# Program order through the first half's q/k stage, and rotation tables made earlier, in an RG-LRU and attention block

## The chip, the cores and the metric

The kernel runs on one core of a Trainium2 chip. The core has a matrix engine (TensorE, PE in the profile, with its weight loads listed apart as PEld), a vector engine (VectorE, DVE), a scalar engine (ScalarE, ACT), a general one (GpSimd, POOL) and an engine that mostly issues transfers (SyncE, SP). They share an on-chip memory; PE writes into a small accumulator memory of eight banks (PSUM). DMA queues move data between the on-chip memory and the chip's main memory (DRAM). Each engine works through its own list of instructions in order, and waits on semaphores for the others.

The metric is the device time of one execution, in microseconds (us). A kernel's time is the median of several runs; beside them one execution is recorded by the hardware profiler.

## The reference

One layer over 2048 positions of width 1024, in float32. The input is normed and modulated, then projected by one weight matrix to eight parts of 1024 columns:

```python
h = rms_norm(x, g_norm[l]) * (1.0 + scale[:, None, :]) + shift[:, None, :]
proj = h @ w_in[l]
x_rnn, z_rnn, q, k, v, z_attn, g_r, g_a = jnp.split(proj, IN_SPLITS, axis=-1)
xc = causal_depthwise_conv(x_rnn, conv_w[l], conv_b[l])
hr = rg_lru(xc, w_a[l], b_a[l], w_x[l], b_x[l], lam[l], positions)
y_rnn = (hr * jax.nn.silu(z_rnn)) @ w_out_rnn[l]
qh = apply_partial_rope(q, cos, sin); kh = apply_partial_rope(k, cos, sin)
o = dilated_attention_mixture(qh, kh, v)
y_attn = (o * jax.nn.silu(z_attn)) @ w_out_attn[l]
merged = sigmoid(g_r + bg_r) * y_rnn + sigmoid(g_a + bg_a) * y_attn
x = x + gate[:, None, :] * (merged @ w_o[l])
```

and a last norm. The rotation (rope) turns the first 32 of each head's 128 columns by the angles positions x inv_freq; its cosine and sine are the same for all 8 heads and for q and k.

## The kernel before

**Tiles and halves.** Activations lie transposed: 128 columns of a result by 512 positions, which is a bank. The 2048 positions are four banks, worked in two halves (f = 0 and 1) of two banks each. Each half has a values stage (v, written as it is used later), a recurrent stage and a q/k stage. Attention, the merge and the output follow after both halves.

**Products.** Float32 is had from PE by splitting every operand in a high and a low part and adding three matmuls. A *pair* is a 256-column piece of the weight matrix times the two banks of the half; it is done by a Strassen scheme with 7 *products* in place of 8. A product is 12 matmuls of 128x512 (4 blocks of the contraction, three parts each) on one weight operand of 128x4x128 in two parts. The products' results go to the PSUM tiles X, Z, W, V and Y and are added up on DVE and ACT (u1, u2, u3, then one eviction for each quarter of the pair); line 440 is such an eviction. A pair's last product is put off into the next pair (`last_product`).

**Operands.** In the first half the weights come from DRAM as raw tiles R (SP, line 243, four to ten products ahead of use), DVE forms the Strassen sums s1 and s2, ACT rounds the high part (line 154) and POOL takes the low part (line 160) into one of seven tiles S, four products ahead; the split operand is also stored to the DRAM array sD (ACT's queue). In the second half the same operands are loaded from sD straight into S (SP, line 307), up to seven ahead, one more each time a product has been issued.

**Stages.** The recurrent stage of a half has 8 recurrent pairs (`recurrent`: conv, two small gate matmuls per block with the weights w_a and w_x, scan, product with the silu gate) and 14 other pairs between them, by the list `others`: gate pairs (z_attn, g_r, g_a; `gate_pairs`) and 2 of the plain pairs. That is 22 pairs, 154 products. The q/k stage has the two *rotated* pairs, which hold the first 32 columns of each head of q and of k, and 4 *plain* pairs, which hold the other columns: 42 products. The rotated results get a lane shuffle (DVE), a product with the cosine table Ct (POOL) and with the sine table St (DVE), and an addition, and go to the arrays qT and kT.

**What lies beside the products.** Before the rotated pairs the q/k stage makes the tables (`rotary_tables`): positions to angles, reduction by 2 pi in 13 exact subtractions (line 890), two sines on ACT, a repeat to 128x512 (rep, line 905), four transposes on PE (line 907) and a copy into Ct or St; rep, transposes and copy four times. In the first half the stage also loads and norms bank 2 of x (line 490), whose transposed and split operands are built during the last pair (`next_even`, line 511); in the second half it makes the residual gate.

**Order.** The program is written in one order; a scheduler then moves instructions on each engine, by its own model of the machine. Exempt from it is only the first half's recurrent loop, which stands in program order on all engines:

```python
with nullcontext() if f else tc.manual_schedule():
    for m in range(KT):
        recurrent(rp, bigr, f, m)
```

Inside it, work that should lie some products later is hung on a counter of products (`steps_after`, the dictionaries `late` and `after_prod`), and `pump` issues the operand events that have come due.

## Time and profile before

| | |
|---|---|
| runs | 2305.05, 2310.1, 2318.68 us (median 2310.1) |
| profiled execution | 2306.3 us, its span 2304.5 |
| granted TensorE clock, mean | 0.987 |

A row of the stage table gives a stretch of the span, then its length, the busy time and count of instructions of PE, weight loads, DVE, ACT and POOL in it, the granted clock (1.00 is full speed), the DMA engines' busy share and what they moved in GB/s. A row of an engine's timeline gives the start, the busy length, the line, the operation with out<-in, and in brackets how long the engine had waited ahead of it and for whom. A row of the chain of waits gives a start, a length and what ran; it follows the work that ended last back through what released each step. A row of DMA issues ends in the size of one and the median time from issue to landing.

### The profile page before, as it was taken

The numbers are of one execution on the slowest core, as the hardware profiler recorded it, in microseconds if no ns is written. First come the engines' busy times: TensorE is split into PE (matmuls) and PEld (weight loads), VectorE is DVE, ScalarE is ACT, GpSimd is POOL, SyncE is SP. The second block draws the span as 40 slices with busy tenths as digits, with TensorE's granted clock in tenths as the row PEclk, the third lists the DMA queues.
The fourth block names the chain that finished last, engine by engine and source line by source line (L and its number), as shares of the span: only waits on it lengthen the run. The fifth ranks groups of instructions, "written<-read, shape, count | busy, mean of one in ns | idle before, by whom it ended". The sixth has DMA issues, their size and how long they took to land.

```text
span 2304.5 us, 34059 instructions
## 1 busy us (share of the span) xinstructions
PE 2230.6 (97%) x11461; PEld 1867.7 (81%) x11461; DVE 1333.6 (58%) x2442; ACT 1242.3 (54%) x2416; POOL 964.6 (42%) x734
## 2 busy tenths in 40 slices
PE   8999999999979999999999999899999998989998
PEld 4998888888858998778888877788888897978886
DVE  4828676867574705343534462466667777667443
ACT  4737666866633636555644411567678777534211
POOL 2457666766545334232111021455556565433000
PEclk9999999999999999999999999999999999999999
DMA  7366888787959388998676779988888887799542
GB/s 264 107 224 245 286 281 280 252 292 272 320 173 311 106 281 303 322 318 297 203 230 229 252 235 301 274 250 277 267 248 247 229 255 233 231 322 284 161 128 92
DMA packets 427284, 569.20 MB, mean 247 GB/s; under 512 B 71943, under 2 KB 292835, under 8 KB 426085
## 3 DMA queue, kind: packets, MB, share of 16 engines
q1 hardware_dynamic: 389268, 447.27, 63.0%
q10 hardware_dynamic: 37648, 119.70, 13.3%
q8 instruction: 91, 1.49, 0.3%
q14 instruction: 85, 0.69, 0.1%
q0 software_dynamic: 192, 0.05, 0.0%
HBM read 355.08 MB, written 211.82 MB: 246 GB/s over the span
## 4 chain that ended last, share of the span: by engine, by line
PE 55%; DMA 8%; DVE 4%; ACT 3%; issue 2%; SPq 2%; POOL 1%; ACTq 0%; POOLq 0%; DVEq 0%
PE pj L146 12%; PE pq L146 8%; PE X L146 8%; PE V L146 7%; PE sc L146 4%; PE o L146 4%; PE Z L146 4%; PE W L146 4%; PE Y L146 3%; DMA wD<-s 1%; PE pT L1299 1%; DMA S<-sD 1%; PE pT L1312 1%; PE pg L146 1%; DMA gaT<-ev 1%
## 5 line engine op out<-in xcount | busy, mean ns | idle before, releaser
L146 PE MATMUL pj<-yh,S 128*128 128x512 f32 x1024 | 370.3, 406 | 4.3 <-DMA S<-wD 2.1
L146 PE MATMUL X<-T,S 128*128 128x512 f32 x1344 | 335.0, 398 | 5.2 <-ACT t L925 2.1
L146 PE MATMUL V<-T,S 128*128 128x512 f32 x1344 | 331.7, 395 | 6.3 <-DVE ev L440 2.7
L160 POOL TENSOR_TENSOR S<-R,S 128x512 fp32r<-128x512 f32 x168 | 251.8, 1510 | 189.6 <-ACT S L154 66.7
L146 PEld LDWEIGHTS X<-T,S 128*128 128x128 f32 x1344 | 254.7, 190 | 66.7 <-ACT t L925 3.1
L146 PEld LDWEIGHTS V<-T,S 128*128 128x128 f32 x1344 | 252.2, 188 | 66.9 <-DVE t L440 5.2
L146 PEld LDWEIGHTS pj<-yh,S 128*128 128x128 f32 x1024 | 194.8, 190 | 41.4 <-DVE fg L1506 2.5
L146 PE MATMUL pj<-yl,S 128*128 128x512 f32 x512 | 202.3, 395 | 0.0
L1215 ACT ACTIVATE pp<-pp,st 128x256 f32<-128x256 f32 (+3 forms) x256 | 133.9, 524 | 112.1 <-DVE st L1214 111.0
L160 POOL TENSOR_TENSOR S<-s,S 128x512 fp32r<-128x512 f32 x84 | 125.9, 1499 | 122.8 <-ACT S L154 96.4
L146 PE MATMUL Z<-T,S 128*128 128x512 f32 x672 | 166.8, 396 | 4.8 <-ACT S L154 4.5
L146 PE MATMUL W<-T,S 128*128 128x512 f32 x672 | 166.0, 395 | 0.3 <-POOL S L160 0.3
L146 PE MATMUL Y<-T,S 128*128 128x512 f32 x672 | 166.2, 395 | 0.0
L146 PEld LDWEIGHTS Z<-T,S 128*128 128x128 f32 x672 | 126.6, 189 | 35.3 <-ACT S L154 4.9
L146 PEld LDWEIGHTS W<-T,S 128*128 128x128 f32 x672 | 126.3, 188 | 30.8 <-issue 0.9
L146 PEld LDWEIGHTS Y<-T,S 128*128 128x128 f32 x672 | 126.2, 188 | 30.3 <-issue 0.9
L812 DVE SCALAR_TENSOR_TENSOR xc<-xr,par,xc 128x512 f32<-128x512 f32 x96 | 92.6, 964 | 78.6 <-ACT xc L806 76.9
L163 DVE TENSOR_TENSOR ptl<-pT,pth 128x384 fp32r<-128x384 f32 (+1 forms) x160 | 97.8, 628 | 64.9 <-ACT pth L154 62.7
L154 ACT ACTIVATE S<-R 128x512 fp32r<-128x512 f32 x168 | 102.3, 623 | 58.6 <-DMA R<-in_w_in_dram 28.2
L1279 ACT ACTIVATE pp<-pp,M 128x256 f32<-128x256 f32 (+3 forms) x256 | 117.9, 523 | 8.8 <-DVE M L1403 8.8
L1214 DVE CUSTOM_DVE_ANT_0 pp<-sc,msk 128x256 f32<-128x256 f32 (+3 forms) x256 | 105.1, 449 | 28.4 <-PE sc L146 25.5
L160 POOL TENSOR_TENSOR vh<-vraw,vh 128x256 fp32r<-128x256 f32 (+1 forms) x64 | 67.4, 1053 | 104.7 <-ACT vh L154 95.0
(357 smaller groups left out, 4697.4 us busy)
## 6 DMA issues: line engine op xcount, KB each, us to landing
sD<-S ACTq DMA_DIRECT2D x196, 512.0 KB, 4.0
S<-sD SPq DMA_DIRECT2D x196, 512.0 KB, 5.6
S<-wD SPq DMA_DIRECT2D x99, 512.0 KB, 5.6
R<-in_w_in_dram SPq DMA_DIRECT2D x136, 256.0 KB, 4.2
wD<-s ACTq DMA_DIRECT2D x64, 256.0 KB, 5.9
T<-in_w_mod_dram SPq DMA_DIRECT2D x8, 1024.0 KB, 11.6
vN<-ev SPq DMA_DIRECT2D x64, 128.0 KB, 2.4
zaT<-ev SPq DMA_DIRECT2D x32, 256.0 KB, 4.6
```

Source lines behind the costliest of these rows:

```text
L146: last_mm[0] = nc.tensor.matmul(o, lhsT=l, rhs=r, start=st, stop=sp, **kw).ins
L154: nc.scalar.activation(o, i, AF.Copy)
L160: nc.gpsimd.tensor_tensor(o, i, h.bitcast(F32), ALU.subtract)
L163: return nc.vector.tensor_tensor(o, i, h.bitcast(F32), ALU.subtract).ins
L812: nc.vector.scalar_tensor_tensor(xc, xr[:, i : i + CH], cw(i), xc, ALU.mult, ALU.add)
L1214: nc.vector.tensor_tensor_reduce(pdst, s_ps, mask, 1.0, 3e38, ALU.add, ALU.min, m_)
L1215: nc.scalar.activation(pdst, pdst, AF.Exp, bias=m_, scale=-1.0, accum_out=l_)
L1279: nc.scalar.activation(pp, pp, AF.Copy, scale=w)
L1299: nc.tensor.transpose(pt[:, c0 + j * P : c0 + (j + 1) * P], pp[i][:, k * P : (k + 1) * P], ident)
L1312: nc.tensor.transpose(pt[:, c * P : (c + 1) * P], pp[:, half * P : (half + 1) * P], ident)
```

## The change

**Order.** The first half's program order no longer ends with the recurrent loop. It is entered at the same place and closed after the q/k stage's last pair. The second half and all else stay with the scheduler.

**Tables.** `rotary_tables` is called at the start of each half's recurrent stage and hangs its work on products: the angles at product 24, then one small group of DVE operations after each product, and the four repeats, transposes and copies at products 56, 76, 91 and 111 and shortly after. The copies go through the tiles `ev` that the gates also use, and to a DRAM array tabD; the q/k stage loads Ct and St from there (`load_tables`).

**Steps of the q/k stage.** What the scheduler placed is now hung on products by hand: the scaling of q one product after the eviction, the shuffle and the turn one and two after that; bank 2's norm in parts (`next_norm`: four squares, one square root for all four, four scalings); the transposes and builds of bank 2 one step apart; the residual gate over some 30 products.

**Small ones.** The recurrent blocks' gate weights are loaded into an `ev` tile in place of one of their own (gr_); the rotated results have one t0 tile more in the first half and one t1 more in both; `others` places the same 14 pairs otherwise (1, 2, 2, 1, 2, 2, 1, 3 behind the eight recurrent ones, before 1, 2, 2, 2, 1, 2, 2, 2); `rstd` works on several rows at once, in as many operations.

```diff
+    def rstd_first(ss):
+
+        nc.vector.tensor_scalar(ss[:, 0], ss[:, 0], 1.0 / D, EPS, ALU.mult, ALU.add)
+        nc.scalar.activation(ss[:, 1], ss[:, 0], AF.Sqrt)
...
         def load_weights():
-            w["raw"] = T(rp, [P, 2, P], F32, "gr_", bufs=1)
+            w["raw"] = T(rp, [P, 4, P], F32, "ev", bufs=3)[:, :2]
...
-    def rotary_tables(qp, f):
+    def rotary_tables(rp, f):
...
+        def piece(q, i):
+
+            def repeat():
+                src = v[("co", "an")[i]]
+                v["rep"] = T(rp, [P, 4, 8, 16], F32, "ev", bufs=3)
+                nc.vector.tensor_copy(v["rep"][:], src[:, 4 * q : 4 * q + 4, :].unsqueeze(2).broadcast_to([P, 4, 8, 16]))
+
+            def turn():
+                v["pt"] = T(pg, [P, 4, P], F32, "pg")
+                for r in range(4):
+                    nc.tensor.transpose(v["pt"][:, r, :], v["rep"][:, r].rearrange("p a b -> p (a b)"), ident)
+
+            def store():
+                t = T(rp, [P, CH], F32, "ev", bufs=3)
+                pt = v["pt"][:].rearrange("p r j -> p (r j)")
+                if i == 0:
+                    nc.scalar.activation(t[:], pt, AF.Copy)
+                else:
+                    nc.vector.tensor_scalar(t[:], pt, cs[:, K_SG : K_SG + 1], None, ALU.mult)
+                nc.sync.dma_start(tabD[f, i, :, q * CH : (q + 1) * CH], t[:])
+
+            return repeat, turn, store
+
+        at_, base = TABLES, n_prod[0]
+        for fn in (angles, None, products, *reduce(TWO_PI * 4096, 7, 8), *reduce(TWO_PI, 11, 5), quarter, sines):
+            if fn:
+                after_prod.setdefault(base + at_, []).append(fn)
+            at_ += 1
+
+        for x, (q, i) in enumerate((q, i) for q in range(2) for i in range(2)):
+            for d, fn in zip((0, 2, 3), piece(q, i)):
+                after_prod.setdefault(base + PIECES[x] + d, []).append(fn)
...
-    NT0 = (3, 5)
+    NT0, NT1 = (4, 5), 3
...
-            if qs != 1.0:
-                nc.scalar.activation(t[:], t[:], AF.Copy, scale=qs)
+        steps_after(n_prod[0], ((1, lambda: nc.scalar.activation(t[:], t[:], AF.Copy, scale=qs)),))
+        return 2
...
+                steps_after(n_prod[0], ((wait, shuffle), (wait + 1, add)))
...
-    others = [1 + (m % 4 > 0) for m in range(KT)]
+    others = [1, 2, 2, 1, 2, 2, 1, 3]
...
+    def next_norm():
+
+        xs = load_x(xp, 2, "x", 2)
+        ss = T(xp, [P, 3, 4], F32, "ss")
...
+        for r in range(4):
+            later(5 + r, lambda r=r: square(r))
+            later(11 + 2 * r, lambda r=r: nc.vector.tensor_scalar(xs[r], xs[r], ss[:, 1, r : r + 1], None, ALU.mult))
+        later(9, lambda: rstd_first(ss))
+        later(10, lambda: rstd_last(ss))
+        return xs
...
+        rotary_tables(rp, f)
...
-        with nullcontext() if f else tc.manual_schedule():
-            for m in range(KT):
+        order = ExitStack()
+        if f == 0:
+
+            order.enter_context(tc.manual_schedule())
+        n = 0
+        for m in range(KT):
...
-        tabs = rotary_tables(qp, f)
+        tabs = load_tables(qp, f)
...
-            x0 = load_x(xp, 2, "x", 2)
-            norm_x(xp, x0)
+            x0 = next_norm()
         rotated_pairs(qp, f, *tabs)
...
+        order.close()
         pools.close("qp")
```

Three places show the order as it now stands. The first is DVE in the first half's q/k stage, where the first rotated outputs (tiles t) are turned. Before (rep, St and co belong to the tables, line 942 and 943 are the turn, 440 an eviction):

```order
L905 COPY rep_5791<-co_5781 128x512
L905 COPY rep_5799<-an_5759 128x512
L913 TENSOR_SCALAR St_5789<-pg_5798,cs_60 128x512
L905 COPY rep_5807<-co_5781 128x512
L942 TENSOR_TENSOR t_1030_5993<-t_1030_5993,St_5789 128x512
L943 TENSOR_TENSOR t_1030_5993<-t_1030_5993,t_1029_5992 128x512
L905 COPY rep_5815<-an_5759 128x512
L440 TENSOR_TENSOR t_1039_6069<-V_5940,u_1016_5914 128x512
```

And now (451 is an eviction, 1007 the shuffle, 1012 and 1013 the turn):

```order
L451 TENSOR_TENSOR t_1022_5927<-V_5906,u_1018_5904 128x512
L1007 STREAM_SHUFFLE t_1029_5968<-t_1022_5927 128x512
L1007 STREAM_SHUFFLE t_1030_5971<-t_1026_5951 128x512
L451 TENSOR_TENSOR t_1033_5981<-Y_5953,u_1018_5904 128x512
L1012 TENSOR_TENSOR t_1029_5968<-t_1029_5968,St_5828 128x512
L1013 TENSOR_TENSOR t_1029_5968<-t_1029_5968,t_1022_5927 128x512
```

The tables' work is gone from between the turns, and an eviction stands between a shuffle and its turn.

The second place is SP at the start of the same stage. Before, with the positions (line 875) and x (490) among the raw weights R:

```order
L243 DMA R_1033_6020<-in_w_in_dram 128x4x96
L875 DMA pi_5755<-in_positions_dram 128x2x4
L490 DMA x_5825<-in_x_dram 128x2048
L490 DMA x_5827<-in_x_dram 128x2048
L243 DMA R_1043_6098<-in_w_in_dram 128x4x64 x2
```

And now, with the tables (975) and x (501):

```order
L975 DMA Ct_5827<-tabD 128x1024
L975 DMA St_5828<-tabD 128x1024
L501 DMA x_5834<-in_x_dram 128x2048
L501 DMA x_5836<-in_x_dram 128x2048
L254 DMA R_1011_5874<-in_w_in_dram 128x4x32 x4
L254 DMA R_1021_5924<-in_w_in_dram 128x4x64 x2
```

The raw weights that stood ahead of x now stand behind it and behind two tables.

The third place is SP in the second half's recurrent stage, where the fourth recurrent block's gate weights are loaded (lines 766 and 767) among the split weights S. Before:

```order
L307 DMA S_1466_8877<-sD 128x1024
L766 DMA gr__1585_9502<-in_w_a_dram 128x128
L767 DMA gr__1585_9502<-in_w_x_dram 128x128
L1030 DMA gaT<-ev_8883 128x512
L307 DMA S_1470_8897<-sD 128x1024
```

And now (783 and 784; 957 stores a piece of the tables):

```order
L318 DMA S_1584_9491<-sD 128x1024
L783 DMA ev_9528<-in_w_a_dram 128x128
L784 DMA ev_9528<-in_w_x_dram 128x128
L957 DMA tabD<-ev_9533 128x512
L1102 DMA zaT<-ev_9476 128x512
L318 DMA S_1592_9523<-sD 128x1024
```

The gate weights go into a tile of the shared ring, with a store of the tables behind them.

More of the change, by code (lines that the diff above doesn't have):

```diff
@@ L1035, in gate_pairs, with later, load, add @@
                 yield
+    def later(d, fn):
+        late.setdefault(n_prod[0] + d, []).append(fn)
     def residual_gate(ep):
         acc = T(ep, [P, D], F32, "gacc")
-        for k in range(KT):
-            t = T(ep, [P, D], F32, "gw", bufs=2)
-            nc.sync.dma_start(t[:], w_mod[0, k * P : (k + 1) * P, 2 * D : 3 * D])
+        row = T(ep, [1, D], F32, "grow")
+        nc.sync.dma_start(row[:], b_mod[0:1, 2 * D : 3 * D])
+        w = {}
+        def load(k):
+            w[k] = T(ep, [P, D], F32, "gw", bufs=2)
+            nc.sync.dma_start(w[k][:], w_mod[0, k * P : (k + 1) * P, 2 * D : 3 * D])
+        def add(k):
+            t = w.pop(k)
             if k == 0:
```

211 lines of the change are left out of this document (121 added, 90 removed).

## The prediction

> **What bounds the kernel now.** I read the first part of the page, then the table by stages, then TensorE's (PE's) own timeline in the stage that loses time, then the chain of work that ended last.
>
> ```profile
> span 2304.5 us, 34059 instructions
> PE 2230.6 (97%) x11461; PEld 1867.7 (81%) x11461; DVE 1333.6 (58%) x2442; ACT 1242.3 (54%) x2416; POOL 964.6 (42%) x734
> ```
>
> PE is the bound, with 73.9 us of idle time. Where that lies is in the stages (columns: stretch, length, busy us and count of PE, weight load, DVE, ACT, POOL; granted clock; DMA share; GB/s):
>
> ```profile
> 150.00:595.00 445.00, 445.00 (x1918) 360.89 (x1917) 322.56 (x338) 304.72 (x488) 305.77 (x207) 1.00 0.79 273
> 595.00:620.00 25.00, 24.63 (x107) 19.66 (x106) 11.05 (x13) 15.85 (x23) 14.06 (x10) 1.00 1.01 325
> 645.00:660.00 15.00, 10.83 (x50) 8.62 (x51) 9.39 (x14) 2.98 (x5) 7.10 (x6) 0.89 0.43 143
> 660.00:685.00 25.00, 18.41 (x70) 14.06 (x69) 20.09 (x27) 4.12 (x7) 13.71 (x10) 0.86 0.60 183
> 596.00:745.00 149.00, 134.62 (x587) 106.77 (x587) 91.14 (x156) 59.56 (x99) 79.28 (x58) 0.97 0.82 266
> 745.00:842.00 97.00, 94.37 (x780) 93.95 (x779) 44.50 (x78) 49.72 (x87) 40.29 (x26) 0.98 0.51 155
> 842.00:1000.00 158.00, 157.12 (x677) 126.58 (x676) 70.35 (x86) 85.98 (x137) 53.53 (x41) 1.00 0.93 317
> 1000.00:1050.00 50.00, 46.47 (x200) 37.06 (x199) 20.79 (x27) 25.32 (x41) 15.45 (x13) 1.00 1.00 345
> 1296.00:1424.00 128.00, 125.45 (x540) 98.89 (x538) 59.90 (x108) 21.82 (x37) 17.37 (x12) 1.00 0.83 269
> ```
>
> 150 to 595 is the first half's recurrent stage, which already stands in program order: PE never idles in it. 596 to 745 is the first half's q/k stage, ordered by the scheduler: 14.4 us idle, clock down to 0.86. 745 to 842 are the second half's values, 842 to 1296 its recurrent stage, 1296 to 1424 its q/k stage. The change touches these alone; the attention and output stages hold the rest of the idle time. PE in the q/k stage of the first half, with the waits in brackets:
>
> ```profile
> 597.00 2.95 PE L146 MATMUL V<-T,S 128*128 128x512 f32 x12
> ...
> 643.80 0.73 PE L146 MATMUL X<-T,S 128*128 128x512 f32 x2 [1.85 <-ACT S L154]
> 645.80 0.95 PE L907 MATMUL pg<-cs,rep 128*128 128x128 f32 x4 [1.27 <-DVE rep L905]
> ...
> 659.10 3.07 PE L146 MATMUL V<-T,S 128*128 128x512 f32 x12 [1.09 <-DVE t L440]
> 666.67 1.22 PE L146 MATMUL Z<-T,S 128*128 128x512 f32 x2 [4.50 <-ACT S L154]
> 669.99 4.57 PE L146 MATMUL X<-T,S 128*128 128x512 f32 x12 [2.09 <-ACT t L925]
> ...
> 739.29 0.60 PE L511 MATMUL pg<-cs,x 128*128 128x128 f32 x4
> 739.65 2.62 PE L146 MATMUL X<-S,T 128*128 128x256 f32 x20
> 742.10 2.94 PE L146 MATMUL V<-T,S 128*128 128x512 f32 x12
> ```
>
> PE waits for split weights (S), for the tables' copies (rep) and for evictions (t). The chain says what made them late, and what an undisturbed product costs:
>
> ```profile
> 591.19 3.69 DMA R<-in_w_in_dram
> 603.62 5.70 DMA R<-in_w_in_dram
> ...
> 619.51 11.15 DMA x<-in_x_dram
> ...
> 959.02 8.03 DMA gaT<-ev
> ...
> 1019.21 9.69 DMA S<-sD
> ...
> 1055.69 2.79 PE Z L146 x12
> ```
>
> **The change, part by part.**
>
> *The order of the first half's q/k stage.* The V of 597.00 is the last of the recurrent stage's 154 products; 42 follow, and the V of 742.10 is the last. 43 products at 2.79 us are 120.0 us. Between them stand 16 table transposes and 28 of the next bank at 0.09 (739.65 less 739.29, by four), 4.0 us, and 23 value matmuls at 0.12 (742.10 less 739.65, by 20), 2.8 us: 126.8 us of clean work. It took 742.10 + 2.79 - 597.00 = 147.9 us. So 21.1 us are lost here: 14.4 idle, and 6.7 of slow clock. That is the most this part can give; PE's work is the same before and after.
>
> In the order on DVE shown with the change, the rotated outputs (t) no longer stand behind the tables' copies (rep), and one product's eviction (line 451) stands ahead of the turn of the one before. On SP, also shown there, the loads of x stood behind the raw weights of the next three operands; now the k pair's last raw weights (R_1011) and the next pair's stand behind two tables and all of x, and x itself waits on SP until PE has left the recurrent stage's memory.
>
> That is the new wait. Sizes and times to landing:
>
> ```profile
> sD<-S ACTq DMA_DIRECT2D x196, 512.0 KB, 4.0
> gaT<-ev SPq DMA_DIRECT2D x32, 256.0 KB, 3.7
> x<-in_x_dram SPq DMA_DIRECT2D x2, 1024.0 KB, 8.8
> ```
>
> Over the two rotated pairs (14 products, 39.1 us) the queues carry 14 x 512 KB of split weights, 8 x 256 raw, 2048 of x, 1024 of tables (2 of 128x1024 f32) and 8 x 256 of outputs: 14336 KB, 14.7 MB. At the 345 GB/s of the row 1000 to 1050 that is 42.6 us, 3.5 too long; at the 325 of 595 to 620, 45.2, 6.1 too long. Against it stands the lead: a weight is split four products (11.2 us) ahead of its use, so lateness up to that does not reach PE. Bounds: 0, and 10 us if the squares of x block ACT in order with the splits behind them. I take 3, near the lower end, since both rates keep the lateness inside the lead. This part: -21.1 + 3 = -18.1 us.
>
> *The tables, now in the recurrent stages.* Per half, by these rows:
>
> ```profile
> L890 DVE SCALAR_TENSOR_TENSOR an<-kk,an x26: 267/286/1114, 629.4 to 1326.7; 128x128 f32<-128x128 f32 x26
> L905 DVE COPY rep<-co x4: 417/417/1491, 644.3 to 1337.7; 128x512 f32<-128x512 f32 x4
> L898 ACT ACT_TABLE_LOAD x1 | 1.3, 1283 | 0.0
> ```
>
> 13 subtractions at 0.286 are 3.7 us, 4 copies 1.7, some 12 more small ones at no more than 0.29, 3.5, and two evictions under 0.8, 1.6: 10.5 us of DVE, spread over products 24 to 114. ACT gets up to two table loads (2.6) and four short operations (under 2). DVE is busy 322.56 of 445 us there and ACT 304.72, so both lie beside PE. PE's 16 transposes (1.4 us) move with them and are in the clean work above, so they cancel. The pieces use the ring of three ev tiles of the gates: a copy may stand for a gate's store to land, 3.7 us on DVE; the accumulators it evicts are wanted again no sooner than two products (5.6 us) later. I take 0; if that cover were gone, 4 x 3.7 = 15; I keep 4, one wait, as the upper end. The eight small stores and the four loads (2 MB more each way over both halves) lie beside the rest.
>
> *The second half.* It stays with the scheduler. Its q/k stage loses 2.55 us idle, and loses the tables' 10.5 us of DVE too; I take -2 (-2.5 to +3). The gate weights' spread (line 1041's loads) and the changed pair order cost nothing that a row shows: same transfers, same products, and DVE has 68 us free. In its recurrent stage the recurrent block's weights come into the ev ring instead of a tile of their own. The order on SP, third place shown with the change, has the fourth such block. The load now also waits for the store that last used its ev tile, and the next split weights, one per product, stand behind it on SP. Seven are loaded ahead, so a single wait is covered, except where DMA is full, at 842 to 1050 (share 0.93 and 1.00), where PE already idles 4.4 us. I take +2 (0 to 12). The values at 745 to 842: the last builds and POOL's splits stand as close as before; 0 (-3 to +3). The merged norm (one Sqrt for four) drops a few DVE operations of 0.2 us, at nothing.
>
> Sum: -18.1 + 0 - 2 + 2 = -18.1 us. On the profiled execution's 2306.3 us (span 2304.5 and 1.8 around it) that is 2288.2. The runs' median, 2310.1, lies 3.8 above that execution, so the forecast for a median is 2292.0.
>
> The clock is the second part of the prize: after the 4.50 us wait the X of 669.99 took 4.57 us where others take 2.95, at a granted 0.86. [...]
>
> **The rivals.**
>
> *Half of it stays, because the stage is bound by its transfers.* For: the chain ahead of 643.80 is DMA of raw weights and of x, and the change puts 1 MB more into it. Against: at 645 to 685 the queues moved only 143 and 183 GB/s while PE idled. At the 266 GB/s of the whole stage 14.7 MB take 55.2 us, 16.1 over; less none to 11.2 us of lead, that is 5 to 16 instead of 3. With 11 the time is 2300: no measurable change.
>
> *Slower: SP blocks in the second half.* Place: the ev ring ahead of the S loads at 842 to 1050, where four of the eight recurrent blocks load weights. A store there takes up to 8.03 us (the chain's gaT). Four such waits reaching PE whole are 32 us, less the 2 counted: 2292 + 30 = 2322. For: full queues there, a wait of 9.69 us on S in the chain. Against: the scheduler placed the load after the S that PE needs next, and seven stand ahead. It is slower by more than the bound once each wait costs PE over 7.9 us (18.1 + 11.6 + 2, by four).
>
> **How the numbers follow.** A measurement here tells 0.5% from nothing, 11.6 us. The forecast, 2292, holds 0.63; the half gain, 2300, 0.23; the blocked queue, 2322, 0.14. The first is faster, the second mostly within 0.5%, the third slower. The range: from 2279 (21.1 + 2.5 + 3 + some 4 of the runs' scatter below 2310.1) to 2307, which takes the forecast with its upper ends (+7 and +4) and all but the worst of the half gain, and leaves out the blocked queue and a few tails.
>
> **What would show it.** In the profile after: the first half's q/k stage 19 to 21 us shorter with a granted clock of 1.00 and PE idle under 3 us; no PE wait for rep; the recurrent stage still 445 of 445. Wrong would be: PE waiting for S behind ACT's squares of x; DVE's shuffle waiting for qT stores; PE idle at 842 to 1050 well over 4.4 us behind S loads; or the values' stage growing by what the q/k stage gave.

## The result, and the profile after

The changed kernel takes 2323.6 us (median of 14 runs, 2319.2 to 2330.0); the kernel before, run beside it, 2309.4 (14 runs, 2300.9 to 2318.7). The ratio is 1.0065, with a 95% interval of 1.0052 to 1.0078. The change made the kernel about 14 us slower, where the forecast said 18 us faster.

The head of the page of the changed kernel:

```profile
span 2322.0 us, 34101 instructions
PE 2233.7 (96%) x11459; PEld 1868.9 (80%) x11461; DVE 1347.5 (58%) x2424; ACT 1238.5 (53%) x2412; POOL 971.1 (42%) x734
```

PE's work is the same, 2233.7 us where it was 2230.6; the span is 17.5 us longer. PE's idle time grew by 14.4 of them, from 73.9 to 88.3 us; the other 3.1 are matmuls that ran longer. To see where it went, both kernels are cut at the same events on PE's own timeline. Of the kernel before: the first product of the first half, the first of the second half, and the first matmul of the attention part. (Where a row counts fewer than the 12 matmuls of a product, the edge of the view cut it.)

```profile
147.81 2.48 PE L146 MATMUL X<-T,S 128*128 128x512 f32 x10
...
842.28 2.94 PE L146 MATMUL X<-T,S 128*128 128x512 f32 x12
...
1424.52 0.47 PE L146 MATMUL pj<-yh,S 128*128 128x512 f32 x1 [0.83 <-issue]
```

The same events after, with the last product of the recurrent stage (609.47; before it was 597.00) and the last one of the first half (750.04; before 742.10) between them:

```profile
150.61 2.94 PE L151 MATMUL X<-T,S 128*128 128x512 f32 x12
...
609.47 2.94 PE L151 MATMUL V<-T,S 128*128 128x512 f32 x12
...
750.04 3.02 PE L151 MATMUL V<-T,S 128*128 128x512 f32 x12
...
849.41 0.85 PE L151 MATMUL X<-T,S 128*128 128x512 f32 x3
...
1445.64 0.47 PE L151 MATMUL pj<-yh,S 128*128 128x512 f32 x1 [0.83 <-issue]
```

The differences of these starts (a product is 2.79 us long) give the account:

| stretch | before | after | difference |
|---|---|---|---|
| up to the first product | 147.8 | 150.6 | +2.8 |
| first half's recurrent stage | 449.2 | 458.9 | +9.7 |
| first half's q/k stage | 147.9 | 143.4 | -4.5 |
| second half's values | 97.4 | 96.6 | -0.8 |
| second half's recurrent and q/k stages | 582.2 | 596.2 | +14.0 |
| attention and output | 880.0 | 876.4 | -3.6 |

The first and the last row are code that the change doesn't touch; in the kernels below that leave the start alone the first lies between 147.6 and 150.6, and the last lies between 872.0 and 882.1 in all of them. Each row is one profiled execution, so 3 us in the first row and 10 in the last are no difference. The stretches between scatter less. The first half's recurrent stage takes 458.9 to 459.9 us in the five kernels that have it as changed (changed, e4, e5, e6, e8). The second half has its instructions in the same order on PE, DVE, ACT and POOL in changed, e4 and e16, and takes 596.2, 598.4 and 597.0. A difference of about 2 us there is not read as one.

The q/k row is not what it seems: most of its 4.5 us is work that now stands elsewhere. The clean work of that stage, counted as in the prediction, was 126.8 us. The 16 table transposes went to the recurrent stage (1.4 of its +9.7 us). Of bank 2's 28 transposes 24 now stand ahead of the last product, and of the 23 value matmuls 10, so the clean work is 123.4 us. Of 147.9 us, 21.1 were lost before; of 143.4, 20.0 are lost now (15.0 idle, the rest slow matmuls). The stage loses nearly as much time as before. The values' -0.8 has the 2.0 us of work in it that moved there.

PE's waits in these stretches of the changed kernel:

```profile
255.79 3.06 PE L151 MATMUL V<-T,S 128*128 128x512 f32 x12 [1.34 <-DVE ev L451]
271.15 4.61 PE L151 MATMUL X<-T,S 128*128 128x512 f32 x12 [3.94 <-ACT u L384]
...
647.94 2.47 PE L151 MATMUL V<-T,S 128*128 128x512 f32 x5 [7.01 <-DVE t L451]
...
677.05 5.18 PE L151 MATMUL V<-T,S 128*128 128x512 f32 x12 [7.50 <-ACT S L159]
...
903.65 4.60 PE L151 MATMUL V<-T,S 128*128 128x512 f32 x12 [3.78 <-DVE ev L451]
...
1033.60 1.09 PE L948 MATMUL pg<-cs,ev 128*128 128x128 f32 x4 [3.67 <-DVE ev L943]
...
1371.19 4.61 PE L151 MATMUL V<-T,S 128*128 128x512 f32 x12 [2.40 <-DVE t L451]
```

In the first half none of the waits of before is there any more, but others came: the recurrent stage, which had none, waits for evictions and for ACT where the tables' steps stand, and the q/k stage waits twice for 7 us. In the second half's products PE idles 14.5 us where it idled 7.5.

**The first half's recurrent stage.** The stretch of 55 us in which the reduction of the angles lies, before, and then after, there with its first 30 us by themselves (columns as in the table of stages):

```profile
222.00:277.00 55.00, 55.00 (x239) 44.59 (x238) 39.30 (x43) 40.23 (x65) 37.92 (x27) 1.00 0.86 300
```

```profile
222.00:252.00 30.00, 29.71 (x129) 23.79 (x128) 29.30 (x39) 20.62 (x31) 16.98 (x12) 1.00 0.72 244
222.00:277.00 55.00, 49.43 (x205) 39.07 (x204) 47.20 (x62) 37.03 (x55) 28.67 (x20) 0.97 0.73 244
```

and DVE's groups of the changed kernel in it (busy, mean ns of one, idle before):

```profile
L921 DVE SCALAR_TENSOR_TENSOR an<-kk,an 128x128 f32<-128x128 f32 x13 | 10.8, 835 | 0.3
...
L866 DVE TENSOR_TENSOR t<-t,gi 128x512 f32<-128x512 f32 x2 | 1.4, 688 | 5.6 <-ACT t L862 5.6
```

The 13 subtractions (line 921) took 835 ns each where the row that priced them had 286, 10.8 us instead of 3.7. They came up to three after one product; DVE was busy for 29.30 of the 30 us from 222 to 252, and the evictions (line 451) stood behind them. (DVE's one long idle time, 5.6 us ahead of line 866, waits for ACT.) Their spread in this half (shortest, median and longest in ns, first and last start in us):

```profile
L921 DVE SCALAR_TENSOR_TENSOR an<-kk,an x13: 278/1262/1378, 236.8 to 256.6; 128x128 f32<-128x128 f32 x13
```

**The first half's q/k stage.** SP, the row of x among the DMA issues, then ACT, at the first wait:

```profile
621.85 3.41 SPq L501 DMA_DIRECT2D x<-in_x_dram  x2
```

```profile
x<-in_x_dram SPq DMA_DIRECT2D x2, 1024.0 KB, 12.8
```

```profile
634.68 1.06 ACT L1154 ACTIVATE hf<-x 128x1024 bf16<-128x1024 f32 x1 [6.86 <-DMA sD<-S]
635.65 0.19 ACT L1154 ACTIVATION_READ_ACCUMULATOR hf<-x 128x1 f32 x1
635.74 0.62 ACT L993 ACTIVATE t<-t 128x512 f32<-128x512 f32 x1
```

The first square of x (line 1154) begins 12.8 us after the load of x was issued, which is the median landing of that load in this stage (12.8, where it was 8.8 before). ACT stands there for 6.86 us; the row names another transfer, the time is that of x. Behind it stand the scaling of q (line 993) and the splits; behind the scaling, on DVE, the turn and then the eviction that PE waits for at 647.94. At the second wait it is DVE itself:

```profile
673.07 1.56 DVE L1013 TENSOR_TENSOR t<-t,t 128x512 f32<-128x512 f32 x1
674.56 1.74 DVE L299 TENSOR_TENSOR s<-R,s 128x512 f32<-128x512 f32 x1
676.22 0.68 DVE L451 TENSOR_TENSOR t<-V,u 128x512 f32<-128x512 f32 x1
```

DVE is busy for 40.5 of the 44 us from 636 to 680, and from 639.15 on it waits for nothing. The sum at 674.56 makes the operand that ACT splits at 676.4 and PE wants since 669.5.

### The profile page after: what moved, and what is told of

The parts are those of the page before. It is cut to its first block, busy times and chain, and to the rows that moved or that the text cites. A ratio compares the mean times of both kernels' runs of the same rounds, so it can differ in the third digit from the quotient of the medians.

```text
span 2322.0 us, 34101 instructions
## 1 busy us (share of the span) xinstructions
PE 2233.7 (96%) x11459; PEld 1868.9 (80%) x11461; DVE 1347.5 (58%) x2424; ACT 1238.5 (53%) x2412; POOL 971.1 (42%) x734
## 3 DMA queue, kind: packets, MB, share of 16 engines
q8 instruction: 91, 1.49, 0.3%
## 4 chain that ended last, share of the span: by engine, by line
PE 50%; DMA 9%; DVE 4%; ACT 3%; issue 2%; POOL 1%; SPq 1%; ACTq 0%; DVEq 0%; POOLq 0%
PE pj L151 11%; PE pq L151 8%; PE X L151 7%; PE V L151 7%; PE o L151 3%; PE Y L151 3%; PE sc L151 3%; PE Z L151 3%; PE W L151 3%; DMA R<-yaT 1%; DMA vraw<-vN 1%; DMA R<-oT 1%; PE pT L1419 1%; PE pg L151 1%; DMA wD<-s 1%
## 5 line engine op out<-in xcount | busy, mean ns | idle before, releaser
L151 PE MATMUL V<-T,S 128*128 128x512 f32 x1344 | 338.7, 401 | 22.6 <-DVE t L451 9.6
L151 PEld LDWEIGHTS V<-T,S 128*128 128x128 f32 x1344 | 257.6, 193 | 86.5 <-ACT S L159 7.9
```

The source lines that it names most:

```text
L151: last_mm[0] = nc.tensor.matmul(o, lhsT=l, rhs=r, start=st, stop=sp, **kw).ins
```

## The experiments

For each run: where the cuts above fall, in us, with the median of its runs and its ratio to the kernel before on the same chip (whose medians there were 2305.8 to 2307.3).

| kernel | first product at | first half's products | values | second half | rest | median | ratio, 95% interval |
|---|---|---|---|---|---|---|---|
| before | 147.8 | 597.1 | 97.4 | 582.2 | 880.0 | 2309.4 | |
| changed | 150.6 | 602.2 | 96.6 | 596.2 | 876.4 | 2323.6 | 1.0065 (1.0052-1.0078) |
| e1 no tables | 150.3 | 591.6 | 96.6 | 586.9 | 875.8 | 2308.4 | 1.0007 (0.9991-1.0023) |
| e2 e1, own gate tile | 148.5 | 590.5 | 96.6 | 585.4 | 876.9 | 2301.3 | 0.9983 (0.9968-0.9998) |
| e3 pairs as before | 147.6 | 599.4 | 96.6 | 598.4 | 876.8 | 2322.2 | 1.0079 (1.0057-1.0100) |
| e4 x later | 148.4 | 596.9 | 96.6 | 598.4 | 874.0 | 2316.9 | 1.0058 (1.0042-1.0075) |
| e5 scheduler in q/k | 148.2 | 598.3 | 95.8 | 597.7 | 881.5 | 2322.3 | 1.0064 (1.0045-1.0083) |
| e6 e4, cosine on DVE | 150.4 | 592.7 | 96.6 | 594.4 | 875.2 | 2312.1 | 1.0024 (1.0012-1.0035) |
| e7 no sines | 150.6 | 596.2 | 96.6 | 598.3 | 880.9 | 2323.7 | 1.0076 (1.0061-1.0091) |
| e8 second half's tables as before | 148.2 | 602.9 | 96.6 | 589.5 | 878.5 | 2316.3 | 1.0041 (1.0025-1.0056) |
| e9 tables in the values stages | 156.5 | 590.5 | 102.5 | 582.9 | 877.3 | 2310.3 | 1.0019 (1.0005-1.0033) |
| e10 e9, repaired | 156.6 | 581.9 | 103.2 | 578.5 | 881.9 | 2301.4 | 0.9976 (0.9961-0.9991) |
| e11 e10, scheduler in q/k | 157.1 | 584.7 | 102.4 | 575.9 | 880.0 | 2303.5 | 0.9980 (0.9963-0.9997) |
| e12 before, tables in the values stages | 155.9 | 587.9 | 101.9 | 578.8 | 881.2 | 2306.6 | 1.0004 (0.9983-1.0026) |
| e13 no reduction | 148.0 | 592.8 | 96.7 | 588.8 | 876.6 | 2306.8 | 1.0012 (0.9997-1.0027) |
| e14 no pieces | 148.4 | 600.4 | 96.7 | 601.3 | 882.1 | 2322.9 | 1.0067 (1.0042-1.0092) |
| e15 e10, tables at the start | 180.5 | 584.4 | 97.2 | 579.2 | 872.0 | 2315.1 | 1.0035 (1.0019-1.0050) |
| e16 reduction spread | 149.2 | 593.2 | 96.6 | 597.0 | 880.5 | 2314.5 | 1.0030 (1.0019-1.0042) |
| e17 e16, repaired | 150.4 | 585.2 | 97.3 | 592.4 | 879.0 | 2299.6 | 0.9972 (0.9958-0.9986) |
| e18 e17, second half's tables as before | 147.9 | 586.2 | 98.9 | 581.5 | 882.1 | 2296.7 | 0.9952 (0.9936-0.9967) |

The first half's products are two stages, and the q/k stage holds different work from kernel to kernel. Its clean work is 43 products at 2.79 us, with the transposes at 0.09 and the value matmuls at 0.12 that the trace has in it; what is left is lost.

| kernel | recurrent stage | q/k stage | clean work | lost |
|---|---|---|---|---|
| before | 449.2 | 147.9 | 126.8 | 21.1 |
| changed | 458.9 | 143.4 | 123.4 | 20.0 |
| e1 | 448.7 | 142.9 | 123.4 | 19.5 |
| e4 | 459.9 | 136.9 | 123.4 | 13.6 |
| e5 | 459.8 | 138.6 | 124.3 | 14.2 |
| e6 | 458.9 | 133.8 | 123.4 | 10.4 |
| e10 | 448.7 | 133.1 | 122.9 | 10.3 |
| e11 | 448.7 | 136.0 | 124.2 | 11.8 |
| e12 | 449.2 | 138.7 | 122.1 | 16.6 |
| e16 | 451.0 | 142.2 | 123.4 | 18.8 |
| e17 | 450.9 | 134.3 | 122.9 | 11.4 |
| e18 | 450.8 | 135.4 | 123.4 | 12.0 |

### Are the tables dear, and where?

```diff
-        rotary_tables(rp, f)
...
-            nc.sync.dma_start(t[:], tabD[f, i])
+            nc.sync.dma_start(t[:], xv[i, 0])
```

> The changed kernel without the making of the rotation tables: all steps of rotary_tables and the stores to tabD are left out, and Ct and St are loaded from rows of x, so q and k are rotated wrongly. Theory A (the tables' small steps and their two sines delay evictions on DVE and ACT in both recurrent stages): the first half's recurrent stage loses its 9.7 us, the second half some 8 to 12 of its 14, and the kernel is at 2303 to 2308. Theory B (the second half is slower by the gate weights' shared tile or by the new order of pairs): the first half still gives back 8 to 10 us, the second half no more than 3, and the kernel is at 2311 to 2316.

The first half's products take 10.6 us less, the second half's stages 9.4 less. Nearly all of the first half's gain is in the recurrent stage, 448.7 us in place of 458.9. That is theory A in both halves, with the median (2308.4) just above its range. In each half 1.4 us of it are the 16 transposes themselves.

```diff
-            w["raw"] = T(rp, [P, 4, P], F32, "ev", bufs=3)[:, :2]
+            w["raw"] = T(rp, [P, 2, P], F32, "gr_", bufs=1)[:]
```

> As the kernel without tables (they are left out here too, and q and k rotated wrongly), and the gate weights again in a tile of their own (gr_) in place of the shared ev ring. Theory A: within 3 us of the kernel without tables. Theory B by the shared tile: 5 to 10 us faster than that kernel, all of it in the second half's recurrent stage.

The stretches fell by 1.2 us in the first half and 1.5 in the second, no more than the same code scatters, so no cost of the shared tile is shown by them. The median fell by 7.1, from 2308.4, of which these stretches explain less than half; the rest is unexplained.

```diff
-    others = [1, 2, 2, 1, 2, 2, 1, 3]
+    others = [1, 2, 2, 2, 1, 2, 2, 2]
```

> The changed kernel with the order of pairs of before (1, 2, 2, 2, 1, 2, 2, 2). Theory A: within 5 us of the changed kernel, 2319 to 2329. Theory B by the order of pairs: the second half gives back 8 us or more, and the kernel is at 2310 to 2316.

The order of pairs gives nothing back in the second half (598.4).

```diff
-        tabs = load_tables(qp, f)
+        tabs = tables_here(qp, f) if f else load_tables(qp, f)
```

(`tables_here` is the rotary_tables of before, and rotary_tables is called in the first half only.)

> The changed kernel with the second half's tables made in its q/k stage as before, the first half's as in the change. Theory A (the second half pays for its early tables): its stages come from 596 to 586 to 589 us, the kernel at 2310 to 2315. Rival (the second half pays for the shared gate tile and the new steps): 593 us or more, 2317 or more.

The second half came to 589.5, just outside the 586 to 589 of theory A: 6.7 of its 14.0 us were its early tables.

### Which part of the tables?

```diff
             for tag in ("an", "co"):
-                nc.scalar.activation(flat(tag), flat(tag), AF.Sin)
+                pass
```

> The changed kernel without the two sines in each half (the tables then hold angles, and q and k are rotated wrongly); the repeats, transposes and copies stay. Theory E (the sines' own table load and the one back to the gates' function hold ACT, and with it the release of an accumulator): the 3.9 us wait at 271 and the slow product behind it go, 5 to 6 us of the first half's recurrent stage, and 5 to 8 us of the second half's; the kernel at 2309 to 2314. Rival (DVE's small steps or the pieces' ev tiles): no more than 4 us in all, 2318 to 2324.

Theory E held for a third of the first half's loss: the wait at 271 fell from 3.94 to 2.12 us and the slow product behind it went (3.05 us in place of 4.61), 3.5 us of the first half's 6.0 being in the recurrent stage. The second half gave nothing, and the median is the rival's, 2323.7.

```diff
-        for fn in (angles, None, products, *reduce(TWO_PI * 4096, 7, 8), *reduce(TWO_PI, 11, 5), quarter, sines):
+        for fn in (angles, None, products, quarter, sines):
```

> The changed kernel without the 13 subtractions and their multiples in each half (angles are clipped, not reduced, so q and k are rotated wrongly); sines and pieces stay. If the DVE steps carry the rest: the first half gives back 4 to 6 us, the second 3 to 8, the kernel at 2310 to 2317. If not: under 2 us in each half, 2318 to 2325.

```diff
-        for x, (q, i) in enumerate((q, i) for q in range(2) for i in range(2)):
-            for d, fn in zip((0, 2, 3), piece(q, i)):
-                after_prod.setdefault(base + PIECES[x] + d, []).append(fn)
```

> The changed kernel without the four repeats, transposes, copies and stores in each half; the reduction and the sines stay, and Ct and St are rows of x (rotation wrong). If the pieces carry the second half's loss (a transpose waits there 3.7 to 5.4 us for its copy, which waits for an ev tile): the second half gives back 5 to 8 us, the first 1.4 to 3, the kernel at 2312 to 2317. If not: under 3 us in each half, 2318 or more.

It is the reduction. Without it the first half gives back 9.5 us, more than expected, and the second 7.4, though the sines and the pieces are still there (the sines some 30 us earlier, at 233.46 in place of 263.28, and PE has no wait in that stage). Without the pieces the first half gives back 1.8 and the second nothing (601.3), though the transpose that waited at 1033 is gone. The sum of the parts left out one by one is not the whole, since each shortens the same queues.

```diff
-            return [multiple] + [lambda i=i: subtract(ccs[i : i + 3]) for i in range(0, n, 3)]
+            return [multiple] + [lambda i=i: subtract(ccs[i : i + 1]) for i in range(n)]
```

> The changed kernel with one subtraction of the reduction after each product in place of three. If the pace is at fault: the first half gives back 5 to 8 of the 9.5 us, the second 2 to 6, the kernel at 2309 to 2317. If the work itself is (DVE stays behind for as long): under 3 us in the first half, 2319 to 2325.

In the first half nearly all of it came back: 593.2 us, 9.1 less, with every instruction still there. The recurrent stage takes 451.0 us, 2.2 more than without tables, and 1.4 of these are the transposes. The stretch of 222 to 277 us in this kernel, and its subtractions:

```profile
222.00:277.00 55.00, 55.00 (x239) 44.59 (x238) 48.57 (x61) 38.30 (x61) 34.83 (x25) 1.00 0.84 284
```

```profile
L921 DVE SCALAR_TENSOR_TENSOR an<-kk,an 128x128 f32<-128x128 f32 x13 | 11.5, 886 | 0.1
```

DVE is busier than in the changed kernel (48.57 against 47.20), and a subtraction as slow; but PE is busy for 55.00 of 55.00. What cost was not DVE's time but how much of it stood in one place ahead of an eviction. One thing is not told apart: the edit also puts the sines eight products later (at 278.86 in place of 263.28), behind the stretch shown, and e7 had the sines at 3.5 us.

In the second half the time is the same (597.0), and this says nothing of the pace. The scheduler orders that half, and it put all of its instructions on PE, DVE, ACT and POOL in the same order as in the changed kernel; the spread never took place there. What the changed kernel's trace does show is the wait at 903.65. The eviction that PE waits for (DVE, 902.91) stands behind a chain of the recurrent block that waits for ACT, and there the sines (line 936) with their table load, and the load back, stand ahead of it:

```profile
894.23 1.28 ACT L936 ACT_TABLE_LOAD   x1
...
896.05 1.28 ACT L862 ACT_TABLE_LOAD   x1
...
898.08 0.69 DVE L866 TENSOR_TENSOR t<-t,gi 128x512 f32<-128x512 f32 x1 [3.28 <-ACT t L862]
```

Without the sines (e7) this wait of 3.78 us is 2.41; without the reduction (e13), which lets the sines come 16 us sooner after the half's first product, or without the tables (e1) it is gone.

### The q/k stage

```diff
-        xs = load_x(xp, 2, "x", 2)
+        later(3, lambda: load(0))
+        later(5, lambda: load(2))
...
-            later(5 + r, lambda r=r: square(r))
+            later(11 + r, lambda r=r: square(r))
```

(The root and the scalings move by six products too.)

> The changed kernel with bank 2's x loaded 3 and 5 products into the first half's q/k stage, behind the raw weights, and squared from product 11 on, in place of at once and from 5. Theory A (ACT stands 6.9 us in front of the first square for the load of x, and splits and scalings stand behind it): the 7.0 us wait of PE at 641 to 648 goes, and its echo in slow clock; the q/k stage is 7 to 12 us shorter, the kernel at 2311 to 2317. Rival (DVE is full there, and PE waits for evictions whatever ACT does): the stage gives no more than 3 us, 2320 to 2325.

The wait of 7.01 us is gone, and the q/k stage is 6.4 us shorter (the first half 5.4), below the 7 expected: waits of 1.49, 1.13 and 0.86 us came up in its place, and the second one stayed at 6.81.

```diff
-                    nc.gpsimd.tensor_tensor(t0[:], t0[:], Ct[:, cq], ALU.mult)
+                    nc.vector.tensor_tensor(t0[:], t0[:], Ct[:, cq], ALU.mult)
```

> The kernel with x later, and the product with the cosine table on DVE in place of POOL. Theory D (DVE is the bound of the rotated pairs because its two-tensor operations take 1.4 to 1.8 us while POOL works, and 0.69 alone): a turned output costs DVE less although it does one operation more, the 6.8 us wait at 670 shrinks below 2 us, and the first half's products take 4 to 8 us less than with x later, the kernel at 2309 to 2313. Rival (DVE's own count of operations bounds, 8 more of 0.69): the wait grows by 2 to 5 us, the kernel at 2318 to 2322.

The 6.81 us wait came down to 1.35, and the first half gained 4.2 us (the q/k stage 3.1), though a wait of 3.85 behind ACT's copy (line 384) appeared. The multiplication with the sine table, all 16 of a kernel (shortest, median, longest in ns), before, after, and here:

```profile
L942 DVE TENSOR_TENSOR t<-t,St x16: 681/692/1796, 651.8 to 1368.7; 128x512 f32<-128x512 f32 x16
```

```profile
L1012 DVE TENSOR_TENSOR t<-t,St x16: 679/1623/1806, 640.4 to 1373.5; 128x512 f32<-128x512 f32 x16
```

```profile
L1012 DVE TENSOR_TENSOR t<-t,St x16: 673/681/689, 634.5 to 1363.5; 128x512 f32<-128x512 f32 x16
```

In the changed kernel 13 of the 16 begin while POOL is at work, on its own product or on a low part (line 165), and take 1.18 to 1.81 us; here none takes more than 0.69. But the turn as a whole did not get cheaper for DVE, which theory D had expected: its three operations take 23.7 us in the first half where e4's two take 22.8, and 16.3 in the second half where two take 16.3. One operation more cost DVE next to nothing. What else changed is that POOL has 66.7 us of work in the q/k stage in place of 80.5, and that DVE no longer waits for POOL's product, as it did in e4 (1.20 and 1.15 us). Which of these freed PE is not told apart.

```diff
         if f == 0:
             order.enter_context(tc.manual_schedule())
...
+        order.close()
         last_product()
...
-        order.close()
```

> The changed kernel with its program order ended after the recurrent loop, as before; all other parts stay, and the scheduler orders the first half's q/k stage. Theory C (program order itself costs there: a late transfer or a full DVE stops all that stands behind it, which the scheduler would have moved ahead): the q/k stage is 7 to 12 us shorter than the changed kernel's 143.4, the kernel at 2309 to 2314. Rival (the steps and transfers of the stage set it, under either order): within 3 us of the changed kernel, 2318 to 2325.

With the scheduler in that stage again the stage is 4.8 us shorter than with program order (the first half 3.9), and the kernel as slow, which is the rival's range. Theory C had 7 to 12: the order costs, but only a part.

### Another place for the tables, and the repairs together

```diff
             for _ in values(vx, m, ws if m == 3 else load_wv(m), n1):
                 next(odd, None)
+            if m == 3:
+                tables_here(vx, f)
```

(with e2's gate tile; `tables_here` makes all of one half's tables and stores them to tabD)

> The changed kernel with the tables made in each half's values stage instead (at its end, by the scheduler's order), and the gate weights in a tile of their own again; the rotation is right. Theory A (the place of the tables' steps costs, not their work): the recurrent stages stand as without tables, first half 590 to 592 us, second half 585 to 588, the values stage 1 to 4 us longer; the kernel at 2301 to 2308. Rival (the work costs the same wherever it stands): 2313 or more.

The recurrent stages are as good as without tables, and 6 to 8 us come up in each values stage instead (1.4 of them the transposes): more than half of what was saved. The kernel is between the two theories. The kernel before with this one part alone tells the same:

```diff
-        tabs = rotary_tables(qp, f)
+        tabs = load_tables(qp, f)
```

> The kernel before with one part of the change alone: the tables made ahead (in the values stage), stored and loaded at the q/k stage; the scheduler's order, the norm and all else as before. By the forecast's reading of that stage (the tables' copies and transposes stand among the turns and cost 4 to 8 of its 21 us): 2298 to 2304. Rival (the stage's loss is x and a full DVE): within 3 us of before, 2304 to 2310.

It gains 9.2 us in the first half's products and 3.5 in the second half, and pays 8.1 and 4.5 in the values: nothing in sum, as the rival had it. About half of the 9.2 is work that stands elsewhere now (the tables' transposes, and the value matmuls, which come behind the last product); the lost time fell from 21.1 to 16.6 us. So the tables did cost the stage of before some 4.5 of its 21 us, within the 4 to 8 expected, and the values paid for it.

```diff
     for j in range(4):
...
+        if j in (1, 2):
+            tables_here(vx, j - 1)
```

(in e10, in place of the values stages)

> The repaired kernel with both halves' tables made at the start of the kernel, among the loads of w_mod, in place of the values stages. If the tables cost only where DVE and ACT have no room: the start stays at 148 to 151 us up to the first product, the second half's values at 96 to 98, products as in the repaired kernel (580 to 583 and 577 to 580); the kernel at 2286 to 2295. Rival (they cost as much here): start 154 us or more, 2298 to 2304.

The start took 180.5 us, 30 more than where no tables are made there. First half, second half and values came near what was expected, but no theory had such a start. At one place DVE stands for the positions, and PE behind it for 7.62 us:

```profile
35.86 0.17 DVE L619 CAST hx<-hx 128x8 f32<-128x8 int32 x1 [9.83 <-DMA hx<-in_positions_dram]
```

That is a part of the 30 us; the rest was not followed up. That DVE was busy for only 77.20 of the 147.8 us of the start in the kernel before did not make the tables free there.

e10 is e9 with the two repairs of the q/k stage, the loads and squares of x still later than in e4, and e11 is e10 with the scheduler in that stage (e5's diff):

```diff
-                    nc.gpsimd.tensor_tensor(t0[:], t0[:], Ct[:, cq], ALU.mult)
+                    nc.vector.tensor_tensor(t0[:], t0[:], Ct[:, cq], ALU.mult)
...
-        xs = load_x(xp, 2, "x", 2)
...
+        later(8, lambda: load(0))
+        later(10, lambda: load(2))
...
-            later(5 + r, lambda r=r: square(r))
+            later(17 + r, lambda r=r: square(r))
```

> As the kernel with tables in the values stage, and x loaded 8 and 10 products into the first half's q/k stage and squared from product 17, the cosine product on DVE. Theory: the repairs add up, the first half's products at 578 to 583 us with PE waits under 6 us, the kernel at 2288 to 2297, faster than both. Rival (the next wait takes their place): first half 586 or more, 2299 or more.

> As the repaired kernel, with the first half's q/k stage left to the scheduler. If program order is worth something once nothing late stands in it: 3 to 10 us slower than the repaired kernel. Rival (order is worth nothing there): within 3 us of it.

e10 has the first half at 581.9 us (15.2 less than before) and beats both kernels, the one before by 0.24% (0.09 to 0.39). The first half and its longest wait (4.99 us) are as expected; the kernel is not, since the start and the second half's values pay 6 to 8 us each. With the scheduler (e11) the first half's products take 2.9 us more, but 1.3 of that is other work in the stage, and the lost time, 10.3 and 11.8, hardly differs; the medians don't separate the two (2301.4 and 2303.5). Program order is worth no more than that there.

e17 puts the same lines on e16, in place of e9. e18 moves x once more and gives the second half its tables and gate tile of before:

```diff
-            w["raw"] = T(rp, [P, 4, P], F32, "ev", bufs=3)[:, :2]
+            w["raw"] = T(rp, [P, 2, P], F32, "gr_", bufs=1)[:] if f else T(rp, [P, 4, P], F32, "ev", bufs=3)[:, :2]
...
-        later(8, lambda: load(0))
-        later(10, lambda: load(2))
+        later(16, lambda: load(0))
+        later(18, lambda: load(2))
...
-            later(17 + r, lambda r=r: square(r))
+            later(22 + r, lambda r=r: square(r))
...
-        rotary_tables(rp, f)
+        if f == 0:
+            rotary_tables(rp, f)
...
-        tabs = load_tables(qp, f)
+        tabs = tables_here(qp, f) if f else load_tables(qp, f)
```

> As the kernel with the reduction spread, and x loaded 8 and 10 products into the q/k stage and squared from product 17, and the cosine product on DVE. If the repairs add up as in the kernel with tables in the values stage: first half 583 to 588 us, start and values stage as in the changed kernel, the kernel at 2295 to 2303, under the kernel before. If DVE's work is the bound: 2304 or more.

> The changed kernel with the reduction spread in the first half, the second half's tables made in its q/k stage as before and its gate weights in a tile of their own, the cosine product on DVE, and x loaded 16 and 18 products into the first half's q/k stage and squared from product 22, behind the rotated pairs. If each repair keeps its worth: first half 579 to 585 us, second half 582 to 587, the kernel at 2287 to 2296, faster than before by 0.5 to 0.9%. Rival (the next in-order wait, of the turn's tile for its store behind raw loads on SP, keeps 5 us or more in the first half): 2297 to 2302.

e17 is 0.28% faster than before, within its expectation; e18 0.48% (0.33 to 0.64), at 2296.7 us the fastest of all. The kernel and its first half missed the 2287 to 2296 and the 579 to 585 us expected by a little, and its waits are of the old kind:

```profile
653.03 4.36 PE L151 MATMUL V<-T,S 128*128 128x512 f32 x12 [3.14 <-ACT S L159]
679.06 4.61 PE L151 MATMUL X<-T,S 128*128 128x512 f32 x12 [2.15 <-ACT u L384]
...
1010.61 4.62 PE L151 MATMUL V<-T,S 128*128 128x512 f32 x12 [2.67 <-DVE ev L451]
```

One more in-order chain showed up in e17, on DVE:

```profile
656.39 0.01 DVE L1007 LOAD_MASK_SELECT t<-t  x1 [4.69 <-DMA qT<-t]
```

A shuffle waited 4.69 us for a tile whose store stood on SP behind raw weights, and PE's wait of 7.70 us, which ended at 660.5, followed.

## Why the prediction was wrong

- **The first half's q/k stage, -18.1 predicted, -4.5 measured,** and 3.4 of these are work that moved to other stages: of the 21.1 us lost, 20.0 are still lost. That the old waits would go was right. The step that failed is the term "I take 3" for what would be late next: 20.0 us came in its place. The prediction named the squares of x blocking ACT, with an end of 10 us, and chose near the other end. The squares made a wait of 7.0 us, shown by moving x (e4, whose stage loses 13.6), and there is a second one of 7.5 that the prediction didn't have, with DVE full of turns beside POOL. Taking the cosine product off POOL brought the second one from 6.81 to 1.35 (e6); whether DVE's or POOL's relief did that is open.
- **The tables, 0 predicted, up to 4 as the worst: +9.7 in the first half,** 1.4 of it the transposes, which the prediction had counted in the other stage. The step that failed is "DVE is busy 322.56 of 445 us there and ACT 304.72, so both lie beside PE". It is an average over the stage, and says nothing of how dense the added work stands: DVE was busy 29.30 of 30 us there, and e16, with more DVE work in the same 55 us but one step a product, had no wait in the stage. And the 13 subtractions, 3.7 us in the sum, were priced at 0.286, the median from the q/k stages; in the recurrent stage, where seven of them began beside a POOL operation, they took 10.8. The copies and the ev ring, for which the 4 us was kept, cost next to nothing in e14 (1.8 us less, its transposes included).
- **The second half, 0 predicted, +14.0 measured.** 6.7 to 8.0 are its early tables (e8 6.7, e13 7.4, e1 9.4 less its transposes). The +2 for the shared gate tile can't be told from nothing (1.5 in e2). About 5 stay unexplained: e2 takes 585.4 where before took 582.2 with 1.4 of transposes in it. How the reduction costs there is shown in part by the wait at 903.65; its subtractions took 0.29 us at the median, and no run here spread them. The rival of a blocked SP, 32 us by four waits, was not it: PE idled 9.9 us from 842 to 1050 in place of 4.4, but no wait of the second half of 0.6 us or more names a load of S.
- **The values of the second half, 0 predicted, -0.8 measured:** right by luck, since 2.0 us of work moved there and its waits fell from 2.6 to 1.4. "The recurrent stage still 445 of 445", one of the signs that were to show the prediction right, shows it wrong: 439.41 (PE's busy time in the same 445 us).
- **The clock:** the product behind a wait of 3.94 took 4.61 us, at a granted 0.63; behind 7.50 it took 5.18, at 0.54; and behind 1.34 it took 3.06, at 1.00. But a wait of 2.40 (1371.19) was enough too: 4.61, at 0.63. Nor had the kernel before slow matmuls behind its longest wait alone: at 646.40, behind waits of 1.85 and 1.27, ten matmuls took 3.95 us where ten take 2.48 (599.79), at a granted 0.61. The length of a wait alone does not say whether the product behind it is slow: behind 2.12 (269.31 in e7) a product took 3.05, behind 2.15 (679.06 in e18) 4.61. What else decides, these rows don't show. That the 6.7 us of slow clock would go with the old waits was an assumption; of the 20.0 us lost now, 5.0 are slow matmuls.

The kernel came out slower by none of the rivals. The half gain was the nearest in kind, since the load of x is behind one of the two long waits.

## What to carry to other kernels

In a list in program order, an engine's share of busy time over a stage says nothing of whether a step fits: count what stands between two instructions that a busy engine waits for, and give each gap one small step. To test that by an edit, look whether the order changed: a scheduler may undo it. A wait for a transfer that was put on an engine in order (the squares of x on ACT, 6.86 us in the changed kernel; a turn's tile on DVE, 4.69 in e17; the positions at the start, 9.83 in e15) stopped all that stood behind it, so its consumer is placed after the measured landing time under that stage's load, not under another's. Work that moves out of a stage is paid for where it goes: measure the gain and the price by stages before taking the sum, and count the work in a stage before calling a shorter stage a gain.

## What the runs showed of the hardware

In the changed kernel the products with the sine table and the sums of the turn (lines 1012 and 1013, 128x512, both operands in the on-chip memory) took 0.67 to 0.69 us when they began while POOL had no operation running (12 of 32), and 1.18 to 1.81 when they began while one ran (19 of 20; the other, begun 0.07 us before the end of POOL's, took 0.68). A short operation shows the difference best. Of the 13 subtractions of 128x128 in the first half, seven began while a POOL operation ran and took 1.26 to 1.38 us, where POOL's operations there took 1.29 to 1.74; six began while none ran and took 0.28 to 0.29. The additions of a product's result to u (line 385, 128x512, one operand in PSUM) took 0.66 to 0.69 us, the 24 that began beside a POOL operation like the 32 that did not. What makes the difference, these times don't show. In e6, with one DVE operation more in place of POOL's, DVE's turns took 23.7 and 16.3 us where they took 22.8 and 16.3 in e4, and the kernel was faster (2312.1 against 2316.9).
